# First weights of the second input pair cast first, the gates' pair put first, and sums and transfers moved

## The chip, the cores and the metric

The kernel runs on one core of a Trainium2 chip. The metric is the device time of one execution in microseconds; the kernel before took 1771.07, 1772.54 and 1774.09 us in three runs, with a median of 1772.54. The engines named here are PE (TensorE, matmul), DVE (VectorE), ACT (ScalarE), POOL (GpSimd) and SP (SyncE, which only issues transfers). Each runs its own instructions in the order in which they were written for it, and waits for the others by semaphores.

## The reference

One step of one layer of a streaming encoder is computed for a prompt of 1024 frames and a sample of 32 frames that share the weights; the model's width is 1024. All is in float32.

```python
h = rms_norm(x, g_mix)
z = h @ w_in
q, k, v, ch, cb, cc, ga, gb = jnp.split(z, SPLITS, axis=-1)
a = attn_core(q, k, v) @ w_attn_out          # windowed attention, 16 heads of 64
u = cc * ch
up = jnp.concatenate([conv_left, u], axis=1)
conv = up[:, 0:n] * conv_w[0]                # three taps
...
bo = (cb * conv) @ w_conv_out
x = x + (jax.nn.sigmoid(ga) * a + jax.nn.sigmoid(gb) * bo) @ w_mix_out
hc = rms_norm(x, g_cross)
...                                          # attention over 256 memory tokens
x = x + co @ w_co
hm = rms_norm(x, g_mlp)
x = x + jnp.square(jax.nn.relu(hm @ w_up)) @ w_down
```

A final norm follows. The tables of keys, values and convolution rows are outputs as well.

## The kernel before, in words

**Frames and products.** The 1056 frames are three chunks of 384, 384 and 288 columns. Features lie on the 128 partitions, in eight blocks. A weight tile is 128 x 1024. A float32 product is made of three passes in a faster format: a weight is split into a high part wh (a cast on ACT, line 120) and the rest wl (a subtraction on DVE, line 121), the activations likewise, and PE adds hi·hi, hi·lo and lo·hi (lines 175 to 177, 877 to 879, 1690 to 1692). So a weight is fetched by SP (wr), cast by ACT, subtracted by DVE, and then used by PE. The tiles wh and wl have three buffers each, wr two.

**Input pairs.** The columns of w_in after queries, keys and values are taken in 15 pairs of tiles (the list XP): C, H and B are the convolution's three inputs, a and b the two gates. A pair's product with chunks 0 and 1 is formed with seven block products instead of eight. For that, sums of weights are made (pair_sums: L866 and L869 give the sum s31, L867 and L868 the sum s24) and sums of operands (x_sums, lines 816 to 823, whose tiles xk are split into the tiles tk and X1 by x_split, lines 834 to 838). A pair has four weight products to be cast: 1 and 2 from the raw weights, 3 and 4 from the sums. Chunk 2 goes plainly into an accumulator pa. The functions x_p1 and x_p2 form the two halves of the first product; between them ACT copies the first half (L920) and the accumulator is then added to. The function x_start begins pairs 0 and 1 while attention ends; x_pair does the rest, and its marks "B11", "W1", "W4", "W3" and "W2" are the places where x_steps casts the next pair's weights.

**What is put into other stages.** The down projection also works with weight sums. They are made in memory beside the attention stage: SP copies tiles (L733), and POOL issues 40 transfers that add to them (L736, list adds), in one slot of attention after the other; each waits for the one before that it builds on. Up pairs (w_up, with key "u") go like input pairs: there, all four instructions of pair_sums were on POOL. In the down projection fold and refold (L1516 to L1526) load operands by POOL's queue, subtract, and store them again, in nine steps that are tied to the products around them.

**What sets the order.** A scheduler with a time model orders each engine's instructions when the program is built; those in pin keep their order. So an edit at one place can move rows in other stages too.

Of the kernel before, what the change touches and what calls it, by code (L numbers as in the profile page):

```python
# [38 lines left out]
def hybrid_step(ctx: ExitStack, tc: tile.TileContext, io):  # L39
    nc = tc.nc  # L40
    act, dve, pool_e, pe, sp = nc.scalar, nc.vector, nc.gpsimd, nc.tensor, nc.sync
# [3 lines left out]
    def nm(s):  # L45
        uid[0] += 1
        return f"{s}_{uid[0]}"
# [399 lines left out]
    def do_K(pr, extras=()):  # L447
        def fn(w):
            kt = at_tile([P, NT], F32, "kt")
            ktt[pr] = kt  # L450
            for c, (o, n) in enumerate(CH):
                a = acc_tile([P, n])
                gemm(a, w, xg[c])
                dve.tensor_mul(kt[:, o : o + n], a, R[c])
                after(extras, c)
            sp.dma_start(io["o_k"][pr], kt[:, 896:])

        return fn
# [22 lines left out]
    def do_Q(kv, j, extras=()):  # L481
        def fn(w):
            for c, (o, n) in enumerate(CH):
                npr = min(n, NPR - o)
                if j == 0:
                    qs[kv, c] = at_tile([P, 4, npr], F32R, "QA" if c < 2 else "QB", 2 if c < 2 else 1)
                    if n > npr:
                        qs[kv, 3] = at_tile([P, 4, n - npr], F32R, "QC", 2)
                a = acc_tile([P, n])
                gemm(a, w, xg[c])  # L490
                t = tmp(n)
                dve.scalar_tensor_tensor(t, a, 0.125, R[c], op0=ALU.mult, op1=ALU.mult)
                parts = [(qs[kv, c], slice(0, npr))]
                if n > npr:
                    parts.append((qs[kv, 3], slice(npr, n)))
                for q, s in parts:
                    for e in range(2):
                        own, other = slice(64 * e, 64 * e + 64), slice(64 - 64 * e, 128 - 64 * e)
                        h = 2 * j + e
                        act.copy(q[own, h], t[own, s])  # L500
                        dve.tensor_sub(q[other, h], t[own, s], q[own, h].bitcast(F32))
                after(extras, c)

        return fn
# [184 lines left out]
    def in_col(tile):  # L689
        which, f = tile  # L690
        return 10 + 8 * "HBCab".index(which) + f
# [34 lines left out]
    def at(slot, fn):  # L726
        events.setdefault(slot, []).append(fn)
# [14 lines left out]
    adds = [x for s in range(len(sums) + 2) for ph in (2, 1, 0) if 0 <= s - ph < len(sums) for x in sums[s - ph][1][ph]]  # L742
# [12 lines left out]
            at(base + 11, lambda kv=kv: do_KS_rest(kv + 1))  # L755
    for i, x in enumerate(copies):
        at(2 + i, x)
    for i, x in enumerate(adds):
        at(8 + i, x)
    at(38, lambda: x_raw(0))  # L760
    at(40, lambda: x_sums(0))
    at(42, lambda: x_raw(1))
# [2 lines left out]
    for i, h in enumerate(h for stage in hosts for h in stage):  # L765
        extras = [(c, e) for c in range(2) for e in events.get(3 * i + c + 1, [])]
        pre = events.get(3 * i, [])
        if h[0] == "Q":
            fn, key = do_Q(h[1], h[2], extras), qt(h[1], h[2])
        elif h[0] == "K":  # L770
            fn, key = do_K(h[1], extras), ("w_in", 8 + h[1])
        else:
            fn, key = do_in(h, extras), ("w_in", in_col(h))
# [28 lines left out]
    def x_raw(k):  # L802
        if k == 0:
            two = [at_tile([P, NT], F32R, t, 2).bitcast(F32) for t in ("KSh", "KSl")]
        elif k == 1:
            two = [C["pool"].tile([P, 1060], F32, tag="u", name=nm("u")), at_tile([P, 4, 256], F32, "bias").rearrange("p h k -> p (h k)")]
        else:
            two = [S["xk"].tile([P, 768], F32, tag="xk", bufs=4, name=nm("xk")) for _ in range(2)]
        xr[k] = b12, b22, b11, b21 = [t[:, a : a + 384] for t in two for a in (0, 384)]
        for t, c, f in ((b12, 1, k), (b22, 1, k + 4), (b11, 0, k), (b21, 0, k + 4)):  # L810
            sp.dma_start(t, io[f"x{c}"][:, f])
# [48 lines left out]
    def pair_sums(key):  # L860
        r1, r2 = raws[key]
        a, b = slice(0, 512), slice(512, 1024)
        s31 = PW["pool"].tile([P, 1024], F32, tag="s31", name=nm("s31"))
        s24 = PW["pool"].tile([P, 1024], F32, tag="s24", name=nm("s24"))
        side = dve if key[0] == "x" else pool_e
        side.tensor_tensor(s31[:, b], r2[:, a], r2[:, b], op=ALU.add)  # L866
        pool_e.tensor_tensor(s24[:, a], r1[:, a], s31[:, b], op=ALU.add)  # L867
        pool_e.tensor_tensor(s24[:, b], r1[:, b], s24[:, a], op=ALU.add)  # L868
        side.tensor_tensor(s31[:, a], r1[:, a], r2[:, a], op=ALU.add)  # L869
        raws[key] += [s31, s24]  # L870
# [13 lines left out]
        issue_w()  # L884


    XP = [((w, f), (w, f + 1)) for f in (2, 4, 6) for w in "CHB"]
    XP.insert(3, (("b", 4), ("b", 5)))
    XP += [(("b", 6), ("b", 7))] + [(("a", f), ("a", f + 1)) for f in (0, 2, 4, 6)]
    LATE = 3  # L890
    xs1, xemit = {}, {}

    def x_fetch(i):
        if i < len(XP):
            pair_fetch(("x", i), *(io["w_in"][in_col(t)] for t in XP[i]))

    def x_issue(i, which):
        if i < len(XP):
            pair_issue(("x", i), which)
        elif which != 2:  # L900
            resume()
# [6 lines left out]
    def x_put(i, half, c, v):  # L908
        tile = XP[i][half]
        if (i, half) not in xemit:  # L910
# [58 lines left out]
    def x_steps(i):  # L969
        if i == 0:  # L970
            todo = {"B11": lambda: x_issue(1, 4), "W4": lambda: x_issue(1, 3), "W2": lambda: [x_issue(1, 2), x_fetch(2), x_issue(2, 1)]}
        elif i == 1:
            todo = {"W4": lambda: x_issue(2, 4), "W3": lambda: x_issue(2, 3), "W2": lambda: x_issue(2, 2)}
        else:
            todo = {f"W{k}": lambda k=k: x_issue(i + 1, k) for k in (1, 4, 3, 2)}
            todo["B11"] = lambda: x_fetch(i + 1)

        def after(what):
            todo.get(what, lambda: None)()
            if what == "B11" and XP[i][0][0] == "a" and "cv_cm" in S:  # L980
                closed(S.pop("r2_cm"))
                closed(S.pop("cv_cm"))
                G["pool"] = ctx.enter_context(tc.tile_pool(name="gb", bufs=5, reuse_waits="tile", side="right"))

        return after

    def x_start():
        x_issue(0, 4)
        A = x_p1(0)
        x_issue(0, 3)  # L990
        x_c2(0, 0)
        x_p2(0, A)
        x_issue(1, 1)
        x_c2(0, 1)
        A = x_p1(1)
        x_p2(1, A)
        x_c2(1, 0)
# [391 lines left out]
    b11, b21, b22 = (lambda k: xm[0][k]), (lambda k: xm[0][k + 4]), (lambda k: xm[1][k + 4])  # L1389
# [125 lines left out]
    def refold(step):  # L1515
        if step % 2 == 0:  # L1516
            if fold:
                for to, k in (("n3", "b22"), ("n1", "b12"), ("t2", "b11"), ("n4", "b21")):
                    pool_e.dma_start(op_d[to][:, step // 2 - 1], fold[k])
            if step < 8:  # L1520
                for k in ("b12", "b22", "b11", "b21"):
                    fold[k] = H["pool"].tile([P, 384], F32, tag="fold", bufs=4, name=nm("fold"))
                    pool_e.dma_start(fold[k], op_d[k][:, step // 2])
        else:
            for to, x, y in (("b22", "b12", "b22"), ("b12", "b11", "b12"), ("b11", "b11", "b22"), ("b21", "b21", "b11")):
                pool_e.tensor_tensor(fold[to], fold[x], fold[y], op=ALU.subtract)  # L1526
# [251 lines left out]
    C11, C12, C21, C22 = (0, 0), (1, 0), (0, 4), (1, 4)  # L1778
    steps = [(j, t) for j in range(4) for t in range(2)]
# [13 lines left out]
    def twos(half, t):  # L1793
        return [h2_of(half, k) for k in range(8 * t, 8 * t + 8)]

    def beside_two(w, kind, then, half, f, begin, more=(), each=None, steps=steps, apart=False):

        for n, (j, t) in enumerate(steps):
            if (j, t) == (3, 1) and more:
                item(lambda: wanted.__setitem__(slice(0, 0), more))  # L1800

            def fn(ws, j=j, t=t, n=n):
                prod(kind, j, t, then)(ws)
                pump(pace(13 - 2 * n))
                if each:
                    each(n)
                two(half, j, t, f, begin, apart)(ws)
                pump(pace(12 - 2 * n))

            item(fn, ("w_down", w, j, t))  # L1810

    def alone(w, kind, then, begin=True, end=True, more=None):
        for j, t in steps:
# [6 lines left out]
            if more and (j, t) == (1, 0):  # L1820
# [1 line left out]

    want(twos(0, 1), ops("b21"))
    beside_two(0, "b11", ((*C12, True, False), (*C21, False, False), (*C22, False, False), (*C11, True, False)), 0, 0, True,
               twos(1, 0), lambda n: n > 3 and refold(n - 4), [(0, 0), (1, 0), (0, 1), (1, 1)] + steps[4:])
    want(twos(1, 1), ops("n4")[4:], ops("n4")[:4])
    beside_two(1, "b21", ((*C11, True, True),), 1, 0, False, each=lambda n: n < 5 and refold(n + 4))
    want(ops("t2"))
    beside_two(3, "n4", ((*C21, True, False),), 1, 4, True, apart=True)
    want(ops("n3"))  # L1830
# [128 lines left out]
```

## Time and profile before

| What | Value |
|---|---|
| Time of the runs, median (lowest to highest) | 1772.54 us (1771.07 to 1774.09) |
| The profiled execution's own time | 1774.1 us |
| Its span in the profile | 1772.3 us |
| Mean granted clock of PE | 0.995 |
| PE busy | 1735.1 us (98%) |
| DVE, ACT, POOL busy | 1203.3, 845.6, 580.0 us |

The span runs from the first to the last recorded work; the profiled execution's own time has 1.8 us around it. A row of a timeline gives start, duration, engine, line, operation, written and read tiles, shape, how many rows were put together, and in brackets the idle time ahead and what ended it. In a row of waits stand who waited, for which engine's write, the sum in us, how often, and the longest one.

### The profile page before, as it was taken

Reading aid. Unit: us, or ns where it says so; the run is one execution under the profiler, and the core shown is the slowest. Engines: PE = TensorE matmul, PEld = TensorE weight load, DVE = VectorE, ACT = ScalarE, POOL = GpSimd, SP = SyncE. Lnnn points to the kernel's source line nnn. Section 1 sums busy time; section 2 is a strip of 40 time slices with the busy share of each in tenths; the row PEclk is TensorE's granted clock in tenths of the full one; section 3 lists DMA queues with packets and bytes.
Section 4 is the critical chain, followed back from the end, with each engine's and each line's share of the span. In section 5 each row is a group of like instructions: output and inputs, shape, how many; then the busy total and the mean of one; then the engine's idle time right before and its main releaser. Section 6 shows DMA issues by size and latency. Waiting matters only on the chain.

```text
span 1772.3 us, 29923 instructions
## 1 busy us (share of the span) xinstructions
PE 1735.1 (98%) x11012; PEld 1714.5 (97%) x11012; DVE 1203.3 (68%) x2114; ACT 845.6 (48%) x1625; POOL 580.0 (33%) x602
## 2 busy tenths in 40 slices
PE   8999999999999999999999999999999999999997
PEld 8999999999999999999999999999999989999997
DVE  6768878677686767457566877676666676444764
ACT  8667767853232335234465755632222343432553
POOL 2245564553232310003324242375555352100111
PEclk9999999999999999999999999999999999999998
DMA  5428997771211325578766777744434496444673
GB/s 183 157 94 237 252 234 197 168 189 56 96 65 56 113 71 187 165 252 297 250 218 210 238 240 227 268 152 147 139 127 138 160 307 219 163 149 141 222 245 128
DMA packets 148547, 317.21 MB, mean 179 GB/s; under 512 B 18320, under 2 KB 101040, under 8 KB 147760
## 3 DMA queue, kind: packets, MB, share of 16 engines
q1 hardware_dynamic: 140448, 287.98, 48.5%
q0 software_dynamic: 7808, 27.27, 7.7%
q8 instruction: 87, 1.43, 0.3%
q14 instruction: 60, 0.49, 0.1%
q10 hardware_dynamic: 144, 0.05, 0.0%
HBM read 254.20 MB, written 98.78 MB: 199 GB/s over the span
## 4 chain that ended last, share of the span: by engine, by line
PE 78%; DMA 7%; DVE 6%; ACT 4%; issue 3%; POOL 2%; SPq 0%; POOLq 0%; DVEq 0%; ACTq 0%
PE acc L175 9%; PE acc L176 9%; PE acc L177 9%; PE acc L877 7%; PE acc L878 7%; PE acc L879 7%; PE acc L1692 5%; PE acc L1690 5%; PE acc L1691 5%; PE pa L176 3%; PE pa L177 3%; PE pa L175 3%; DVE wl L121 2%; DMA ct<-bc_d 1%; PE pt L587 1%
## 5 line engine op out<-in xcount | busy, mean ns | idle before, releaser
L120 ACT CAST wh<-wr 128x1024 fp32r<-128x1024 f32 (+1 forms) x224 | 234.3, 1046 | 312.2 <-PE acc L1691 89.0
L121 DVE TENSOR_TENSOR wl<-wr,wh 128x1024 fp32r<-128x1024 f32 (+1 forms) x224 | 306.9, 1370 | 103.7 <-ACT wh L120 102.4
L175 PE MATMUL acc<-Y,wh 128*128 128x384 f32 (+1 forms) x624 | 201.7, 324 | 0.7 <-DVE ct L1333 0.4
L176 PE MATMUL acc<-Y,wh 128*128 128x384 f32 (+1 forms) x624 | 201.9, 323 | 0.0
L177 PE MATMUL acc<-Y,wl 128*128 128x384 f32 (+1 forms) x624 | 201.7, 323 | 0.0
L175 PE MATMUL acc<-X,wh 128*128 128x384 f32 (+1 forms) x528 | 172.5, 327 | 0.1
L176 PE MATMUL acc<-X,wh 128*128 128x384 f32 (+1 forms) x528 | 171.3, 324 | 1.0 <-DVE X L256 1.0
L177 PE MATMUL acc<-X,wl 128*128 128x384 f32 (+1 forms) x528 | 171.0, 324 | 0.0
L252 POOL TENSOR_TENSOR xacc<-xacc,ct 128x384 f32<-128x384 f32 (+1 forms) x62 | 78.1, 1260 | 270.1 <-ACT ct L250 267.7
L175 PEld LDWEIGHTS acc<-Y,wh 128*128 128x128 f32 x624 | 117.2, 188 | 1.3 <-DVE ct L1333 0.7
L177 PEld LDWEIGHTS acc<-Y,wl 128*128 128x128 f32 x624 | 117.3, 188 | 0.0
L176 PEld LDWEIGHTS acc<-Y,wh 128*128 128x128 f32 x624 | 117.2, 188 | 0.0
L577 POOL TENSOR_SCALAR S<-S,rec 128x256 f32<-128x256 f32 (+1 forms) x96 | 90.3, 956 | 80.9 <-DVE rec L574 80.9
L1692 PE MATMUL acc<-Y,wl 128*128 128x384 f32 (+1 forms) x352 | 113.1, 321 | 2.6 <-DVE wl L121 2.6
L1690 PE MATMUL acc<-Y,wh 128*128 128x384 f32 (+1 forms) x352 | 113.1, 321 | 0.6 <-ACT wh L120 0.6
L1691 PE MATMUL acc<-Y,wh 128*128 128x384 f32 (+1 forms) x352 | 113.0, 321 | 0.0
L120 ACT CAST wh<-s 128x1024 fp32r<-128x1024 f32 x54 | 56.6, 1051 | 107.1 <-PE acc L878 69.6
L176 PEld LDWEIGHTS acc<-X,wh 128*128 128x128 f32 x528 | 100.0, 189 | 2.7 <-DVE X L256 1.8
L175 PEld LDWEIGHTS acc<-X,wh 128*128 128x128 f32 x528 | 99.9, 189 | 1.7 <-ACT wh L120 0.3
L177 PEld LDWEIGHTS acc<-X,wl 128*128 128x128 f32 x528 | 99.8, 189 | 0.6 <-DVE wl L121 0.2
L1118 POOL TENSOR_TENSOR sgl<-sgl,ct 128x384 f32<-128x384 f32 (+1 forms) x21 | 22.2, 1055 | 224.5 <-DVE sgl L1115 166.5
L121 DVE TENSOR_TENSOR Y<-ct,Y 128x384 fp32r<-128x384 f32 (+1 forms) x128 | 71.6, 591 | 31.4 <-ACT Y L120 31.0
(413 smaller groups left out, 5321.0 us busy)
## 6 DMA issues: line engine op xcount, KB each, us to landing
wr<-in_w_in SPq DMA_DIRECT2D x55, 512.0 KB, 3.4
wr<-in_w_up SPq DMA_DIRECT2D x48, 512.0 KB, 3.7
wsum_d<-in_w_down SPq DMA_DIRECT2D x32, 512.0 KB, 6.4
wr<-in_w_down SPq DMA_DIRECT2D x32, 512.0 KB, 3.5
wr<-wsum_d SPq DMA_DIRECT2D x32, 512.0 KB, 3.5
wl<-wl_d SPq DMA_DIRECT2D x28, 512.0 KB, 4.8
wsum_d<-in_w_down POOLq DMA_DIRECT2D x24, 512.0 KB, 7.9
wr<-in_w_conv_out SPq DMA_DIRECT2D x24, 512.0 KB, 4.7
```

Source lines behind the costliest of these rows:

```text
L120: act.copy(hi, src)
L121: dve.tensor_sub(lo, src, hi.bitcast(F32))
L175: pe.matmul(out, wh[:, a], hi, start=(k == 0), stop=False)
L176: pe.matmul(out, wh[:, a], lo, start=False, stop=False)
L177: pe.matmul(out, wl[:, a], hi, start=False, stop=(k == len(acts) - 1))
L577: pool_e.tensor_scalar_mul(stl[:, h, :nk], stl[:, h, :nk], rec[:, h : h + 1])
L877: pe.matmul(acc, wh[:, a], hi, start=(start and k == 0), stop=False, skip_group_check=True)
L878: pe.matmul(acc, wh[:, a], lo, start=False, stop=False, skip_group_check=True)
L879: pe.matmul(acc, wl[:, a], hi, start=False, stop=(k == 3), skip_group_check=True)
L1690: pe.matmul(a, wh[:, s], hi, start=(start and k == 0), stop=False, skip_group_check=True)
L1691: pe.matmul(a, wh[:, s], lo, start=False, stop=False, skip_group_check=True)
L1692: pe.matmul(a, wl[:, s], hi, start=False, stop=(stop and k == len(acts) - 1), skip_group_check=True)
```

## The change

It has five edits:

- x_start casts the first weights of pair 1 before all else, and the third weights of pair 0 only after pair 0's two halves.
- In the list XP, the pair of gate tiles (b4, b5) becomes pair 0; the three pairs C, H and B of tiles 2 and 3 become 1 to 3. The other pairs keep their places.
- Of the 40 transfers that add to the sums of w_down, the first 30 stay in attention's slots; the last ten are issued one each at the end ("W2") of input pairs 1 to 10.
- For up pairs 0 and 1, L866 and L869 are on DVE and no longer on POOL; L867 and L868 stay on POOL.
- The steps of refold begin one product later.

```diff
-    for i, x in enumerate(adds):
-        at(8 + i, x)
+    for i in range(30):
+        at(8 + i, adds.pop(0))
...
-        side = dve if key[0] == "x" else pool_e
+        side = dve if key[0] == "x" or key[1] < 2 else pool_e
...
-    XP = [((w, f), (w, f + 1)) for f in (2, 4, 6) for w in "CHB"]
-    XP.insert(3, (("b", 4), ("b", 5)))
+    XP = [(("b", 4), ("b", 5))]
+    XP += [((w, f), (w, f + 1)) for f in (2, 4, 6) for w in "CHB"]
...
             todo.get(what, lambda: None)()
+            if i and what == "W2" and adds:
+                adds.pop(0)()
...
     def x_start():
+        x_issue(1, 1)
         x_issue(0, 4)
         A = x_p1(0)
-        x_issue(0, 3)
         x_c2(0, 0)
         x_p2(0, A)
-        x_issue(1, 1)
+        x_issue(0, 3)
         x_c2(0, 1)
         A = x_p1(1)
         x_p2(1, A)
...
-               twos(1, 0), lambda n: n > 3 and refold(n - 4), [(0, 0), (1, 0), (0, 1), (1, 1)] + steps[4:])
+               twos(1, 0), lambda n: n > 4 and refold(n - 5), [(0, 0), (1, 0), (0, 1), (1, 1)] + steps[4:])
...
-    beside_two(1, "b21", ((*C11, True, True),), 1, 0, False, each=lambda n: n < 5 and refold(n + 4))
+    beside_two(1, "b21", ((*C11, True, True),), 1, 0, False, each=lambda n: n < 6 and refold(n + 3))
```

Two lines are added ahead of x_start, so line numbers above 980 are higher by two after the change.

**ACT, at the start of the input pairs.** Before, the cast of pair 1's first weights (wh_5149 from the raw tile wr_5046) stands here, among the casts of operand sums; the last row is the next weight cast of pair 0 or 1, of a sum s:

```order
L120 CAST wh_5083<-s_936_4982 128x1024
L120 CAST wh_5102<-s_935_4981 128x1024
L920 COPY s_960_5100<-acc_5087 128x384
L834 CAST tk_4881<-xk_4864 128x384
L834 CAST X_945_5034<-xk_4864 128x384
L834 CAST tk_4885<-xk_4863 128x384
L834 CAST tk_4889<-xk_4863 128x384
L834 CAST tk_4993<-xk_4870 128x384
L834 CAST tk_4997<-xk_4869 128x384
L120 CAST wh_5149<-wr_5046 128x1024
```

After the change (the same cast is wh_5073 from wr_5036) it stands in the attention stage, ahead of the first operand sums' casts:

```order
L604 COPY tO_4707<-o_4701 64x512
L120 CAST PTh_888_4720<-pt_4718 128x128
L120 CAST wh_5073<-wr_5036 128x1024
L834 CAST X_903_4815<-KSl_4253 128x384
L677 ACTIVATE ct_4938<-ct_4938 128x288
```

and farther down, where it stood, comes the third cast of pair 0 (wh_5141 from the sum s_935), followed by two sigmoids (L677) and the copy of pair 1's first half:

```order
L834 CAST tk_4987<-xk_4860 128x384
L120 CAST wh_5141<-s_935_4971 128x1024
L834 CAST X_947_5028<-xk_4861 128x384
L834 CAST tk_4991<-xk_4860 128x384
L677 ACTIVATE ct_5137<-ct_5137 128x384
L677 ACTIVATE ct_5170<-ct_5170 128x288
L920 COPY s_971_5187<-acc_5174 128x384
```

So the cast of pair 1 moved ahead by some 25 rows, and the casts of pair 0's third weights and the copies are now behind sigmoids of the gates.

**PE, at the same place.** Before, after the end of pair 0 (pa_5153) there are two rows of pair 1's first product and two of its chunk 2, and then the products with tk begin:

```order
L176 MATMUL pa_5153<-X_105_580,wh_955_5079 128x288
L177 MATMUL pa_5153<-X_104_579,wl_956_5080 128x288
L877 MATMUL acc_5181<-X_10_173,wh_5149 128x384
L878 MATMUL acc_5181<-X_11_174,wh_5149 128x384
L175 MATMUL pa_5212<-X_90_551,wh_5149 128x288
L176 MATMUL pa_5212<-X_91_552,wh_5149 128x288
L877 MATMUL acc_5251<-tk_4812,wh_5083 128x384
```

After, all 48 rows of pair 1's first product (acc_5174, both halves) and its chunk 2 (pa_5204) stand ahead of the products with tk. These are the last rows of them:

```order
L176 MATMUL pa_5204<-X_105_580,wh_5073 128x288
L177 MATMUL pa_5204<-X_104_579,wl_5074 128x288
L877 MATMUL acc_5174<-X_18_193,wh_5073 128x384
L878 MATMUL acc_5174<-X_19_194,wh_5073 128x384
L879 MATMUL acc_5174<-X_18_193,wl_5074 128x384
...
L879 MATMUL acc_5174<-X_24_205,wl_5074 128x384
L877 MATMUL acc_5242<-tk_4803,wh_5077 128x384
```

Pair 1's first product is no longer split around the products with tk.

**POOL, at the sums of the second up pair.** Before, all four of them stand here:

```order
L1408 TENSOR_TENSOR xacc_9095<-xacc_9095 128x384
L866 TENSOR_TENSOR s_2711_13861<-wr_2679_13621 128x512
L869 TENSOR_TENSOR s_2711_13861<-wr_13620,wr_2679_13621 128x512
L1340 TENSOR_TENSOR ct_13813<-ct_13811 128x288
L867 TENSOR_TENSOR s_2712_13862<-wr_13620,s_2711_13861 128x512
L1408 TENSOR_TENSOR xacc_9095<-xacc_9095 128x384
L868 TENSOR_TENSOR s_2712_13862<-wr_13620,s_2712_13862 128x512
```

and after, two:

```order
L1410 TENSOR_TENSOR xacc_9091<-xacc_9091 128x384
L867 TENSOR_TENSOR s_2712_13858<-wr_13616,s_2711_13857 128x512
L1342 TENSOR_TENSOR ct_13809<-ct_13807 128x288
L868 TENSOR_TENSOR s_2712_13858<-wr_13616,s_2712_13858 128x512
L1410 TENSOR_TENSOR xacc_9091<-xacc_9091 128x384
```

L866 and L869 have gone to DVE's queue; what is left of the pair's sums on POOL follows the addition to xacc at once. The fold's rows (L1516 to L1526) stand in the same order among the others as before, on PE, POOL and SP.

## The prediction

> **What bounds the kernel now.** I read the page first, then the waits of PE (columns: who waited, for whom, us in total, times, longest), then stretches of time.
>
> ```profile
> PE 1735.1 (98%) x11012; PEld 1714.5 (97%) x11012; DVE 1203.3 (68%) x2114; ACT 845.6 (48%) x1625; POOL 580.0 (33%) x602
> ```
>
> ```profile
> PE acc L877 <- ACT wh L120: 5.6, 3, 3.6
> ...
> PE o L599 <- DVE AO L606: 0.9, 1, 0.9
> ```
>
> TensorE is busy in 1735.1 of 1772.3 us and the change leaves its work as it is: as many matmuls, of the same shapes. So only PE's 37 us of idle time and its clock can move. The top row says that a weight cast on ScalarE is the costliest wait: three times, 3.6 us the longest. I looked for the place (columns: stretch, its length, busy us and instructions of PE, PEld, DVE, ACT, POOL, granted PE clock, DMA share, GB/s):
>
> ```profile
> 385.00:390.00 5.00, 1.91 (x13) 1.68 (x11) 5.00 (x7) 1.37 (x3) 2.39 (x3) 0.96 0.55 100
> 390.00:395.00 5.00, 4.45 (x14) 4.45 (x15) 5.00 (x7) 1.68 (x4) 4.82 (x4) 0.50 0.04 8
> 395.00:400.00 5.00, 5.00 (x26) 5.00 (x26) 2.07 (x3) 1.01 (x3) 3.23 (x3) 0.85 0.29 105
> 400.00:405.00 5.00, 5.00 (x36) 5.00 (x35) 0.52 (x2) 0.48 (x1) 0.31 (x2) 1.00 0.00 0
> ```
>
> The stall is at the start of the input pairs, and the next stretch shows a second loss that no wait lists: the clock is 0.50. PE, one by one:
>
> ```profile
> 386.62 0.29 PE L177 MATMUL pa<-X,wl 128*128 128x288 f32 x1
> 390.56 0.69 PE L877 MATMUL acc<-X,wh 128*128 128x384 f32 x1 [3.64 <-ACT wh L120]
> ...
> 391.84 0.52 PE L877 MATMUL acc<-tk,wh 128*128 128x384 f32 x1
> ...
> 396.32 0.41 PE L879 MATMUL acc<-tk,wl 128*128 128x384 f32 x1
> 396.57 0.34 PE L877 MATMUL acc<-tk,wh 128*128 128x384 f32 x1
> ...
> 398.66 0.33 PE L879 MATMUL acc<-X,wl 128*128 128x384 f32 x1
> ```
>
> From 396.57 to 398.66 are 12 steps, 0.174 us each. From 391.84 to 396.57 are 15 steps of the same shape, 4.73 us where 2.61 would do: 2.12 lost. The four matmuls between 390.56 and 391.84 (two of 384 columns, two of 288, together 0.62 at full rate) took 1.28: 0.66 lost. The stall thus costs 3.64 + 2.78 = 6.4 us. Why the cast is late, on ScalarE and VectorE:
>
> ```profile
> 388.63 0.92 ACT L834 CAST tk<-xk 128x384 fp32r<-128x384 f32 x2 [4.79 <-DVE xk L822]
> 389.46 1.04 ACT L120 CAST wh<-wr 128x1024 fp32r<-128x1024 f32 x1
> ```
>
> ```profile
> 387.46 1.14 DVE L822 SCALAR_TENSOR_TENSOR xk<-xk,prm,xk 128x384 f32<-128x384 f32 x1
> 388.99 0.68 DVE L866 TENSOR_TENSOR s<-wr 128x512 f32<-128x512 f32 x1
> ```
>
> The cast needs nothing from VectorE; it stands behind two casts of tk that wait 4.79 us for L822, and VectorE is busy 5.00 of 5.00 us there.
>
> **The change part by part.** *First weights first, gates first (x_start, XP).* The order rows ahead of this show wh of pair 1 cast behind the last PTh cast, where ScalarE was near 364 us. Its raw weights were fetched long before:
>
> ```profile
> 339.17 0.38 SPq L845 DMA_DIRECT2D wr<-in_w_in  x1
> ```
>
> So the 3.64 wait and the slow clock behind it go: −6.4. By 386.77 PE has done the same of pair 0 as now, and goes straight on with pair 1: 12 matmuls of 384 columns, 24 of 288 (0.13 each by their columns), 12 of 384, 7.3 us in all, and reaches the tk products near 394.1.
>
> What is late next? Those last 12 (near 392.0) add to an accumulator that ScalarE's L920 must have copied first. That copy now stands behind the cast of wh for pair 0's W3, two tk casts and two sigmoids, and the second sigmoid waits for a VectorE product that stands behind wl of W3. The rows this hangs on:
>
> ```profile
> 379.70 1.98 ACT L120 CAST wh<-s 128x1024 fp32r<-128x1024 f32 x2
> 381.71 0.48 ACT L920 COPY s<-acc 128x384 f32<-128x384 f32 x1
> ```
>
> ```profile
> 383.37 1.37 DVE L821 SCALAR_TENSOR_TENSOR xk<-xk,prm,xk 128x384 f32<-128x384 f32 x1
> 384.67 2.03 DVE L121 TENSOR_TENSOR wl<-s,wh 128x1024 fp32r<-128x1024 f32 x1
> ```
>
> VectorE after L821 (384.7) runs two tk subtractions and a product (about 0.5 each), L822 and L823 (0.6 to 1.1 each): 387.6. Two casts on ScalarE (0.92) and the wh cast (1.04) end at 389.6; wl (1.2 to 2.0) ends at 390.9 to 391.7, the product at 391.3 to 392.1, sigmoid and copy about 1 us later: 392.2 to 393.0, an estimate. PE would wait 0.2 to 1.0 us; I take 0.4, near its lower end. If VectorE and GpSimd slow each other as in the 2.03 us row above, it is up to 2.6. The first product of pair 1's W4 comes at 398.7; By estimate L866 and L869 follow wl on VectorE until 393.4, GpSimd's two sums end near 395.5, the cast near 396.6, wl at 397.8 to 398.6: in time, 0 taken. So **x_start: −6.0, between −6.4 and −3.8**.
>
> [...]
>
> *Ten adds of the w_down sums out of attention (adds).* PE waits 0.94 us in the attention stage for a VectorE that is held up by a load:
>
> ```profile
> 349.25 0.62 DVE L821 SCALAR_TENSOR_TENSOR u<-bias,prm,u 128x384 f32<-128x384 f32 x1 [4.03 <-DMA bias<-in_x]
> ```
>
> ```profile
> 352.08 0.47 PE L599 MATMUL o<-PTh,VS 128*128 128x512 f32 x1 [0.94 <-DVE AO L606]
> ```
>
> L606, for which PE waits, stands two instructions behind. The load competes with the adds that now come later, and has to land 0.94 us sooner for all of the wait to go. Bounds 0 and −0.94; −0.7, nearer the full end since 0.94 is little beside the 4.03 that L821 waits. Where the adds go:
>
> ```profile
> 450.00:800.00 350.00, 350.00 (x2194) 350.00 (x2193) 231.71 (x325) 121.27 (x180) 54.11 (x50) 1.00 0.39 127
> ```
>
> ```profile
> POOL s L867 <- issue: 98.3, 8, 17.8
> ```
>
> ```profile
> L736 POOL DMA_DIRECT2D wsum_d<-in_w_down x24: 794/870/1445, 143.5 to 385.6; - x24
> ```
>
> PE has no gap in these 350 us, GpSimd is busy 54 of them, and before the sums of a pair (L867) it idles 12 us on average (98.3 over 8, from 400 to 700 us). An add holds it 0.87 us (median of min/median/max in ns): hidden, 0. Without that cover ten would cost 8.7. The sums are read in the down projection, some 800 us later.
>
> *First up pairs' sums shared (side).* The wait at the second up pair:
>
> ```profile
> 1175.80 1.29 POOL L866 TENSOR_TENSOR s<-wr 128x512 f32<-128x512 f32 x1
> 1177.05 1.28 POOL L869 TENSOR_TENSOR s<-wr,wr 128x512 f32<-128x512 f32 x1
> ```
>
> ```profile
> 1182.27 1.04 ACT L120 CAST wh<-s 128x1024 fp32r<-128x1024 f32 x1 [5.47 <-POOL s L868]
> ```
>
> ```profile
> 1183.37 0.44 PE L877 MATMUL acc<-hx,wh 128*128 128x384 f32 x1 [1.07 <-ACT wh L120]
> ```
>
> GpSimd loses 2.57 us ahead of L868; VectorE does the two in 0.68 each (the L866 row above). L868 comes up to 2.6 us sooner, the cast too: −1.07, bounds 0 and −1.07. The first pair's L866 now stands ahead of some of VectorE's Gb products at 1126, where PE waits already: +0.7 at most, +0.2 taken.
>
> *Fold one step later.* The fold's instructions stand in the same order with and without it on every engine: they are tied by their data. 0.
>
> *Down projection.* Nothing there is edited, but the rows move: two weight casts come two rows and one row later behind casts of H, and three fetches of weights one or two rows later behind ct loads.
>
> ```profile
> 1446.03 1.04 ACT L120 CAST wh<-wr 128x1024 fp32r<-128x1024 f32 x1
> ...
> 1461.38 1.06 ACT L120 CAST wh<-wr 128x1024 fp32r<-128x1024 f32 x1 [0.88 <-DMA wr<-in_w_down]
> ```
>
> ```profile
> 1449.30 0.44 PE L1692 MATMUL acc<-Y,wl 128*128 128x384 f32 x1 [1.56 <-DVE wl L121]
> ```
>
> One H cast more ahead of 1446.03 makes that cast some 0.46 us later (two such casts are 0.92 above), and the wait behind it grows by as much; a fetch of weights that the cast at 1461.38 already waits for, behind a late load, could make 2.5. The cast that another one leaves free comes sooner: −0.5 at the other end. I take +0.5, nearest to one cast.
>
> **Sum:** −6.0 − 0.7 − 1.07 + 0.2 + 0.5 = −7.1; ends −6.4 − 0.94 − 1.07 − 0.5 = −8.9 and −3.8 + 0.7 + 2.5 = −0.6. The profiled execution took 1774.1, span 1772.3; the runs have a median of 1772.54, 1.6 below it. 1774.1 − 7.1 = 1767.0 for such an execution, **1765.4 us** for the median.
>
> **Rivals.** *The idle only moves (A).* The L920 copy comes 2.5 to 4 us late because VectorE is saturated until 395. For it: DVE 5.00 of 5.00 in two stretches, and the new chain through wl, product and sigmoid; against: wl of pair 1 has left that stretch. Gain 6.4 − 3 + 1 = 4.4, 1768; past 3.6 us idle the slow clock returns as well and about 1 us is left: 1771.5.
>
> *The slow clock is not the idle's (B)*, but comes with this stretch. Against it: the matmul behind the wait of 1.56 us takes 0.44, not the 0.52 of the slow stretch. Gain 3.64 + 0.7: 1768.
>
> *Something given back in up and down (C):* the terms at their bad ends, gain 2 to 3: 1770.
>
> *The moved adds hold GpSimd (D), slower.* Each add waits for the one before to land, and L867 and L868 of a pair are queued behind it, then a cast, then PE.
>
> ```profile
> wsum_d<-in_w_down POOLq DMA_DIRECT2D x24, 512.0 KB, 7.9
> ```
>
> A pair is 132 matmuls, of 2194 in 350 us: 21 us long. At 7.9 us to land an add doesn't wait; it decides once landing takes 12 us more than a pair, about 33 us. Then every pair past that loses; 1.5 us on each of ten is +15, less 7: 1780. [...] Against it is the L736 row: never over 1.45 us.
>
> **Chances.** Forecast 0.68, A 0.18, B 0.05, C 0.04, D 0.05. Of A 0.10 gains over 0.2% (3.5 us, about what can be told from no change here), of B 0.04, of C 0.01; so faster 0.82, same 0.08 + 0.01 + 0.03 + 0.01 for the forecast's bad end = 0.13, slower 0.05. The sum's ends from the median are 1763.6 and 1771.9; the range goes 1.7 us lower, for the spread of the runs, and stops at 1771.0, with most of A and C in: 1761.9 to 1771.0.
>
> **What would show it.** Right: no wait over 1.5 us and clock 1.00 from 385 to 400; no PE wait on AO near 352, none on wh near 1183. A wait of PE on ScalarE's L920 copy, 0.2 to 1 us, near 392. Clock 0.50 without an idle above 3 us is B; L867 waiting behind L736 is D; new rows near 1450 and 1465 are C. I am wrong if the first tk product doesn't come 6 us sooner.

## The result, and the profile after

The changed kernel takes 1763.99 us (median of four runs, 1760.33 to 1765.63) against 1772.08 for the kernel before (four runs): a ratio of 0.995, 95% interval 0.9932 to 0.9969. That is 8.1 us less. The profiled execution took 1763.26 us, its span 1761.5, mean granted clock 0.995. In line numbers above 980 two have to be taken off to find them in the kernel printed above.

The page's first part and two rows of PE's waits, after:

```profile
PE 1734.7 (98%) x11012; PEld 1714.6 (97%) x11012; DVE 1202.1 (68%) x2118; ACT 846.8 (48%) x1625; POOL 575.6 (33%) x594
```

```profile
PE acc L1693 <- DVE H L121: 1.9, 4, 0.7
...
PE acc L877 <- ACT wh L120: 0.5, 1, 0.5
```

PE's work is the same (every kernel here has the three passes, so what a product in another format takes isn't shown); its idle time went from 37.2 to 26.8 us (1761.5 − 1734.7). The row that was the top one, PE waiting for a weight cast (5.6 us), is down to 0.5, and the wait on AO is gone from the list. Pair 1's first weights are now cast in the attention stage:

```profile
362.57 1.05 ACT L120 CAST wh<-wr 128x1024 fp32r<-128x1024 f32 x1 [1.74 <-PE acc L176]
```

and the start of the input pairs reads so (the same stretches as before; columns as there):

```profile
385.00:390.00 5.00, 5.00 (x36) 5.00 (x35) 4.96 (x9) 3.94 (x8) 2.29 (x2) 1.00 0.20 69
390.00:395.00 5.00, 5.00 (x32) 5.00 (x31) 2.29 (x3) 2.33 (x4) 4.92 (x5) 1.00 0.12 33
395.00:400.00 5.00, 5.00 (x30) 5.00 (x30) 2.17 (x2) 0.00 (x0) 0.63 (x1) 1.00 0.29 105
400.00:405.00 5.00, 4.35 (x26) 4.03 (x25) 3.88 (x7) 2.13 (x3) 0.43 (x1) 1.00 0.00 0
```

Where 1.91 and 4.45 of 5 us were busy at clocks of 0.96 and 0.50, PE is now busy throughout at clock 1.00; the first gap, 0.65 us, comes at 401.70.

To see where in the program time goes, PE's 11012 matmuls of a trace were put in order of time and the n-th of them set beside the n-th of the trace of before (median over 17 neighbours). The table gives the difference in us at times of before's trace; a step from one line to the next is what that stretch gained (down) or lost (up). The second column is another execution of the changed kernel, the rest are the experiments below.

| before's time | after | after, again | start + gates | adds | sums | after less sums | late fold, less sums |
|---|---|---|---|---|---|---|---|
| 349.6 | −0.5 | −0.1 | 1.5 | −0.1 | 0.3 | −0.5 | 0.5 |
| 353.4 | −1.7 | −1.3 | 1.3 | −1.2 | −0.8 | −1.6 | −0.7 |
| 385.9 | −1.6 | −1.2 | 1.3 | −1.2 | −0.8 | −1.6 | −0.6 |
| 412.2 | −7.7 | −7.2 | −4.0 | −3.5 | 0.1 | −7.6 | −6.6 |
| 825.2 | −8.4 | −8.0 | −4.8 | −3.5 | 0.0 | −8.4 | −7.2 |
| 832.3 | −10.2 | −9.9 | −6.7 | −5.0 | −1.8 | −10.3 | −8.0 |
| 1114.5 | −11.2 | −9.9 | −6.6 | −4.2 | −2.3 | −10.6 | −7.9 |
| 1208.6 | −9.9 | −9.2 | −6.6 | −2.8 | −1.9 | −10.9 | −7.3 |
| 1431.8 | −9.9 | −9.2 | −6.6 | −2.7 | −1.7 | −10.8 | −7.3 |
| 1444.6 | −5.6 | −9.4 | −5.1 | −1.7 | −1.6 | −10.2 | −9.4 |
| 1471.2 | −9.3 | −11.3 | −6.6 | −1.2 | −3.3 | −11.0 | −13.2 |
| 1755.4 | −9.3 | −11.3 | −6.6 | −1.2 | −3.3 | −11.0 | −13.2 |

The change gains 1.2 us at the attention wait (349.6 to 353.4) and 6.1 at the start of the input pairs (385.9 to 412.2). Nearly all columns gain 1 to 2 us more between 825 and 832, the kernel with an unchanged order (below) too: there the profiled execution of before had 1.3 us of waits that no other profile has:

```profile
828.44 0.45 PE L175 MATMUL acc<-M,wh 128*128 128x384 f32 x1 [0.44 <-ACT M L120]
829.76 0.44 PE L176 MATMUL acc<-M,wh 128*128 128x384 f32 x1 [0.88 <-DVE M L121]
```

That isn't the change's, nor are the 1.5 to 1.8 us by which every other profile is shorter than before's behind the last matmul (the span of after is 10.8 us shorter, where the table ends at −9.3). With these two, before's 1774.1 lies 2.0 us above the median of 1772.08.

### The profile page after: what moved, and what is told of

Its sections match the earlier page's. It is cut to its first block, busy times and chain, and to the rows that moved or that the text cites. A ratio compares the mean times of both kernels' runs of the same rounds, so it can differ in the third digit from the quotient of the medians.

```text
span 1761.5 us, 29915 instructions
## 1 busy us (share of the span) xinstructions
PE 1734.7 (98%) x11012; PEld 1714.6 (97%) x11012; DVE 1202.1 (68%) x2118; ACT 846.8 (48%) x1625; POOL 575.6 (33%) x594
## 4 chain that ended last, share of the span: by engine, by line
PE 88%; DMA 4%; DVE 3%; ACT 2%; issue 2%; POOL 1%; SPq 0%; POOLq 0%; DVEq 0%; ACTq 0%
PE acc L175 11%; PE acc L176 11%; PE acc L177 11%; PE acc L877 7%; PE acc L879 7%; PE acc L878 7%; PE acc L1693 6%; PE acc L1694 6%; PE acc L1692 6%; PE pa L176 3%; PE pa L175 3%; PE pa L177 3%; PE pt L587 2%; DMA wr<-in_w_up 1%; DVE wl L121 1%
## 5 line engine op out<-in xcount | busy, mean ns | idle before, releaser
L121 DVE TENSOR_TENSOR Y<-ct,Y 128x384 fp32r<-128x384 f32 (+1 forms) x128 | 67.4, 559 | 36.9 <-ACT Y L120 36.2
```

Source lines behind the costliest of these rows:

```text
L121: dve.tensor_sub(lo, src, hi.bitcast(F32))
```

## The experiments

The kernel before had medians of 1772.73, 1771.40 and 1772.89 us in the three sessions. Each ratio is to it, in the same session.

**The start of the input pairs together (start + gates).** Before with the new order of x_start and the new XP:

```diff
-    XP.insert(3, (("b", 4), ("b", 5)))
+    XP = [(("b", 4), ("b", 5))]
+    XP += [((w, f), (w, f + 1)) for f in (2, 4, 6) for w in "CHB"]
...
+        x_issue(1, 1)
         x_issue(0, 4)
         A = x_p1(0)
-        x_issue(0, 3)
         x_c2(0, 0)
         x_p2(0, A)
-        x_issue(1, 1)
+        x_issue(0, 3)
```

> The kernel before with two edits alone: the new x_start and the gates' pair first. Theory (stage by stage): the stall of 3.64 us on the late cast and the slow clock behind it are one loss of 6.4 us, and these two edits alone remove it; median 6 to 7.5 us below before, clock 1.00 from 385 to 400 us, the 0.94 us wait near 352 still there, 1.07 at the second up pair still there. Rival: the ten moved adds are needed for the gain too, since POOL and the transfers make VectorE late there; then at most 4 us. In the prediction ScalarE's copy of pair 1's first half was to cost PE 0.2 to 1.0 us.

Measured: 1765.98 us, 0.9965 (0.9952 to 0.9977). PE's only wait from 385 to 412 us is this one; it stands in the changed kernel as well, at 401.70:

```profile
405.30 0.44 PE L877 MATMUL acc<-X,wh 128*128 128x384 f32 x1 [0.65 <-DVE lt L950]
```

The clock is 1.00 from 385 to 400 us. Most of the change's gain is this.

**The two apart.** First only the order of x_start, then only XP:

```diff
+        x_issue(1, 1)
         x_issue(0, 4)
...
+        x_issue(0, 3)
         x_c2(0, 1)
```

> The kernel before with the new x_start alone; the first pair stays C2, C3. Theory: the early cast of pair 1's first weights is what removes the stall, so most of the two edits' gain of 6.2 us is here: 5 to 7 us below before, no wait on that cast. Rival: the gates' pair first is needed too, since the convolution's products keep VectorE and POOL busy at that place and another wait of 1 to 3 us takes the stall's place; then 2 to 4 us below before.

Measured: 1770.38 us, 0.9995 (0.9981 to 1.0009). The stall isn't gone, it has moved. PE, then the stretch around it, then POOL in this kernel:

```profile
405.73 0.45 PE L877 MATMUL acc<-tk,wh 128*128 128x384 f32 x1 [1.57 <-ACT wh L120]
406.99 0.69 PE L879 MATMUL acc<-tk,wl 128*128 128x384 f32 x1 [0.64 <-DVE wl L121]
```

```profile
405.00:410.00 5.00, 3.63 (x11) 3.31 (x12) 2.75 (x4) 1.19 (x2) 1.01 (x1) 0.66 0.29 108
```

```profile
392.06 0.81 POOL L736 DMA_DIRECT2D wsum_d<-in_w_down  x1
392.98 1.05 POOL L629 TENSOR_TENSOR Ga<-Ga,R 128x288 f32<-128x288 f32 x1
396.13 1.26 POOL L629 TENSOR_TENSOR Ga<-Ga,R 128x384 f32<-128x384 f32 x1 [2.10 <-DVE Ga L628]
...
401.96 1.28 POOL L867 TENSOR_TENSOR s<-wr,s 128x512 f32<-128x512 f32 x1
403.32 1.28 POOL L868 TENSOR_TENSOR s<-wr,s 128x512 f32<-128x512 f32 x1
```

PE now waits for pair 1's fourth weights: their sum on POOL (L867, L868) stands behind a transfer, splits of operand sums (L838) and the products of L629, one of which waits 2.10 us for VectorE. This is the longest of the ten executions, 1775.64 us: ahead of the edit's place it has lost 5.2 us on before already, with a wait of 2.36 on AO at 355.86. So it shows which wait comes next, not what a median execution gains.

```diff
-    XP = [((w, f), (w, f + 1)) for f in (2, 4, 6) for w in "CHB"]
-    XP.insert(3, (("b", 4), ("b", 5)))
+    XP = [(("b", 4), ("b", 5))]
+    XP += [((w, f), (w, f + 1)) for f in (2, 4, 6) for w in "CHB"]
```

> The kernel before with the gates' pair first alone; x_start as before. Theory: the cast still stands behind the tk casts and these wait for VectorE, so the stall stays (3 us or more, clock 0.50 behind it): within 1.5 us of before. Rival: gates need less of VectorE at the start of the pairs than the convolution's products, so the tk chain and the cast are earlier, the idle falls under some 2 to 3 us, the clock stays up: 3 to 5 us below before.

Measured: 1771.48 us, 1.0002 (0.9987 to 1.0017); the stall is as it was:

```profile
391.36 0.69 PE L877 MATMUL acc<-X,wh 128*128 128x384 f32 x1 [4.05 <-ACT wh L120]
```

So neither part alone is worth anything that can be measured (the intervals reach some 3 us either way), and the two together are worth 6.8 us by their medians. In the changed kernel the same two sums follow the operands' sums with nothing of L629 or L736 between, and the cast is in time:

```profile
390.77 1.75 POOL L867 TENSOR_TENSOR s<-wr,s 128x512 f32<-128x512 f32 x1
392.60 1.29 POOL L868 TENSOR_TENSOR s<-wr,s 128x512 f32<-128x512 f32 x1
```

They start some 11 us sooner. Of these 6.8 are only that the one execution is 5.2 us behind before's at 385.9, and the other 1.6 ahead; the remaining 4 or so are the order.

**The changed kernel with the old XP**, to see whether moving the adds does for the start what the gates do:

```diff
-    XP = [(("b", 4), ("b", 5))]
-    XP += [((w, f), (w, f + 1)) for f in (2, 4, 6) for w in "CHB"]
+    XP = [((w, f), (w, f + 1)) for f in (2, 4, 6) for w in "CHB"]
+    XP.insert(3, (("b", 4), ("b", 5)))
```

> The changed kernel with C2, C3 as pair 0 again (no gates' pair first). From the run of the new x_start alone: GpSimd's three products L629 of the convolution stand ahead of the sums L867, L868 of pair 1, so PE waits for the cast of the fourth weights. Theory: that is the gates' whole part; a wait of 1 to 2.5 us on that cast is back near 400 us, and the time is 2 to 5 us above the changed kernel. Rival: with the ten adds out of the way GpSimd has room enough; within 1 us of the changed kernel.

Measured: 1766.74 us, 0.9969 (0.9954 to 0.9983); the changed kernel, run again beside it (its text below), had 1764.85, 0.9962 (0.9949 to 0.9974). In its trace the stretch from 385.9 to 412.2 gains 4.7 us instead of 6.1, with a wait of 0.64 for wl at 398.49 and none for the cast. The intervals overlap: start with adds has most of what start with gates has, and the rest, about 2 us, isn't settled.

> The changed kernel as it is, once more, as the base for the three runs beside it: 1762 to 1766 us. If the slow stretch of PE's clock in its down projection (near 1428 to 1433 us in the first profile) belongs to this order of instructions, it is there again; if it was one execution's, it isn't.

**Is the slow clock the idle time's?** (rival B). Before, with the second half of pair 0's chunk 2 computed twice, so that PE has 24 more matmuls of 288 columns to do in the idle (3.1 us at 0.13 each; the first result is overwritten):

```diff
-    def x_c2(i, half):
+    def x_c2(i, half, again=False):
...
         gemm(a, x_w(i, 1 + half), xg[2])
+        if again:
+            gemm(a, x_w(i, 1 + half), xg[2])
...
-        x_c2(0, 1)
+        x_c2(0, 1, again=True)
```

> The kernel before, but chunk 2 of pair 0's second tile is multiplied twice in x_start (24 more matmuls of 288 columns, 3.2 us, the same result), so that PE works through most of its idle 3.64 us without anything else moving. Theory (the slow clock follows from the idle time): the wait on the cast falls to about 0.4 us, the clock stays 1.00 from 390 to 400, the products with tk run at 0.174 us each: 2 to 3 us below before with more work done. Rival (the slow clock comes with this stretch, from transfers or power, whatever PE did before): clock 0.50 again, time as before or up to 0.5 us more.

Measured: 1766.93 us, 0.9979 (0.9968 to 0.999): faster with more work. This kernel's PE and its stretches:

```profile
391.54 0.44 PE L877 MATMUL acc<-X,wh 128*128 128x384 f32 x1 [0.74 <-ACT wh L120]
394.43 0.45 PE L878 MATMUL acc<-tk,wh 128*128 128x384 f32 x1 [0.24 <-DVE tk L836]
397.66 0.44 PE L879 MATMUL acc<-X,wl 128*128 128x384 f32 x1 [1.62 <-DVE wl L121]
```

```profile
390.00:395.00 5.00, 4.02 (x24) 3.30 (x22) 5.00 (x7) 2.42 (x5) 3.85 (x3) 1.00 0.23 45
395.00:400.00 5.00, 3.38 (x20) 3.06 (x20) 3.43 (x4) 1.57 (x4) 4.24 (x4) 1.00 0.23 80
```

The wait on the cast is 0.74, the clock 1.00, and the stretch is the same one, with VectorE as saturated until 395. B falls: before, the clock was 0.50 behind 3.64 us of idle, and in the same stretch it is 1.00 where 0.74 us of it are left. How the whole gain comes about isn't shown. Two more waits follow here, so that the idle is 2.60 instead of 3.64 and the added work takes 3.1; this execution (1771.39, the second-longest of the ten) gains only 0.3 us from 385.9 to 412.2, set beside before's matmul by matmul without the 24. No trace shows one near the median.

**The adds alone:**

```diff
-    for i, x in enumerate(adds):
-        at(8 + i, x)
+    for i in range(30):
+        at(8 + i, adds.pop(0))
...
+            if i and what == "W2" and adds:
+                adds.pop(0)()
```

> The kernel before with one edit alone: the last ten adds issued in the input pairs. Theory: the load that VectorE waits for near 342 us lands sooner, the 0.94 us wait of PE near 352 goes, nothing is lost in the pairs (PE without a gap there, L867 never held by an add): median 0.7 to 1.3 us below before. Rival (the adds hold GpSimd): gaps of PE in the pairs, median above before by up to 15 us. Second rival (the wait at 352 isn't the adds'): no change, 0.94 stays.

Measured: 1769.01 us, 0.9978 (0.9969 to 0.9987), some 3.7 us where 0.7 was predicted. The wait at 352 us goes (1.1 in the table), and part of the big stall's cost goes with it, without an edit there:

```profile
387.73 0.44 PE L877 MATMUL acc<-X,wh 128*128 128x384 f32 x1 [2.04 <-ACT wh L120]
391.22 0.44 PE L878 MATMUL acc<-tk,wh 128*128 128x384 f32 x1 [0.85 <-DVE tk L836]
394.47 0.44 PE L879 MATMUL acc<-X,wl 128*128 128x384 f32 x1 [0.43 <-DVE wl L121]
```

```profile
385.00:390.00 5.00, 2.96 (x18) 2.73 (x18) 5.00 (x6) 2.64 (x5) 3.77 (x4) 1.00 0.00 0
390.00:395.00 5.00, 3.72 (x20) 2.91 (x19) 4.88 (x6) 1.43 (x4) 5.00 (x4) 1.00 0.00 0
```

The wait on the cast is 2.04 instead of 3.64, and the clock stays at 1.00. Two waits follow that before doesn't have, so that the idle is 3.32 in all; the 2.3 us that this stretch gains in the table are thus mostly the clock's. The casts of tk ahead of the first wait, which wait for VectorE, come 2.8 us sooner, 1.6 more than the 1.2 by which all is earlier (why VectorE gets there sooner wasn't tried by itself):

```profile
385.80 0.92 ACT L834 CAST tk<-xk 128x384 fp32r<-128x384 f32 x2 [3.27 <-DVE xk L822]
```

Start with gates and adds thus remove the same stall, and their gains don't add: 6.8 and 3.7 alone, 8.1 for all five edits. For the attention wait, the load that L821 waited 4.03 us for holds it up 0.19 in the changed kernel:

```profile
345.22 0.62 DVE L821 SCALAR_TENSOR_TENSOR u<-bias,prm,u 128x384 f32<-128x384 f32 x1 [0.19 <-DMA bias<-in_x]
```

and in the pairs the ten cost nothing. The 350 us in which they now stand, after:

```profile
450.00:800.00 350.00, 350.00 (x2193) 350.00 (x2192) 236.89 (x335) 122.84 (x181) 66.24 (x64) 1.00 0.48 144
```

GpSimd is busy 12 us more, PE has no gap. Rival D falls.

**The sums alone, and the change without them:**

```diff
-        side = dve if key[0] == "x" else pool_e
+        side = dve if key[0] == "x" or key[1] < 2 else pool_e
```

> The kernel before with one edit alone: two of the four sums of the first two up pairs on VectorE. The prediction's theory: the 1.07 us wait on wh at the second up pair goes, up to 0.2 comes back at the first pair, 0.5 is lost in the down projection: median 0.3 to 0.9 us below before. Rival, from the trace after the change: the wait only changes its name (on ScalarE's copy L1401 and VectorE's subtraction L1433 at the same places), and the down projection's weight casts come later: no gain in the up pairs, median 0 to 1.5 us above before.

> The changed kernel without the edit of the up pairs' sums. The prediction's theory: the 1.07 us wait is back, median about 0.4 us above the changed kernel (which is at 1764.0). Rival: that edit costs more than it brings, and this one is 0 to 2 us below the changed kernel; in the down projection the casts stand as in the kernel before, and the stretch from 1424 to 1434 us of the changed kernel with many short gaps and a clock of 0.61 to 0.71 isn't there.

Measured: alone 1771.67 us, 0.9998 (0.9988 to 1.0008); the change without them 1763.92, 0.9949 (0.9937 to 0.9961). They gain nothing that can be measured, though the intervals, some 2 us either way, wouldn't exclude the forecast 0.9. The traces do: the wait of 1.07 near 1183 has others in its place. The changed kernel at the first and the second up pair, and then the one without the sums' edit:

```profile
1157.12 0.45 PE L877 MATMUL acc<-Y,wh 128*128 128x384 f32 x1 [0.75 <-ACT s L1403]
1172.95 0.45 PE L879 MATMUL acc<-hx,wl 128*128 128x384 f32 x1 [0.51 <-DVE wl L121]
1177.70 0.44 PE L877 MATMUL acc<-hx,wh 128*128 128x384 f32 x1 [0.65 <-DVE lt L1435]
```

```profile
1172.52 0.44 PE L877 MATMUL acc<-hx,wh 128*128 128x384 f32 x1 [1.35 <-ACT wh L120]
```

With the sums on DVE, it is wl and lt, written by DVE itself, that PE waits for at the second pair, 1.11 to 1.19 us together in all five profiles with the edit. At the first pair all five have a wait of 0.75 to 0.93 on ScalarE's copy (L1403), which is at most 0.20 without the edit. So by the traces the edit costs a little.

**The fold alone.** On every engine the rows stand in the same order as before:

```diff
-               twos(1, 0), lambda n: n > 3 and refold(n - 4), [(0, 0), (1, 0), (0, 1), (1, 1)] + steps[4:])
+               twos(1, 0), lambda n: n > 4 and refold(n - 5), [(0, 0), (1, 0), (0, 1), (1, 1)] + steps[4:])
...
-    beside_two(1, "b21", ((*C11, True, True),), 1, 0, False, each=lambda n: n < 5 and refold(n + 4))
+    beside_two(1, "b21", ((*C11, True, True),), 1, 0, False, each=lambda n: n < 6 and refold(n + 3))
```

> The kernel before with the fold's steps one later alone. The instructions and waits of every engine stand as in the kernel before, so both theories say no change; the difference that is measured, at most 1.5 us either way, is what an edit of no effect looks like, and its trace shows how far the stages of one program differ from one execution to another.

Measured: 1772.88 us, 1.0006 (0.9996 to 1.0017). Nothing, as the unmoved rows say.

**The fold really delayed.** In the changed kernel GpSimd loads the fold's operands as soon as they are in memory, and subtracts beside VectorE's splits of H, for which PE waits: 1.9 us in the list above. So the first four loads were made to wait for the last H tile, by a copy of one element per partition into the tile that the load then overwrites; once on the changed kernel, and once without the sums' edit.

```diff
                     fold[k] = H["pool"].tile([P, 384], F32, tag="fold", bufs=4, name=nm("fold"))
+                    if step == 0:
+                        pool_e.tensor_copy(fold[k][:, 0:1], h2[0][15][1][:, 0:1].bitcast(F32))
```

> The changed kernel, but the fold really starts later: four one-element copies on GpSimd from the last H tile of the first half are put ahead of its first loads, so these wait until that tile has been split. Theory: the fold's loads and GpSimd's subtractions are what makes the H tiles late in the down projection (their splits take 0.8 to 0.9 us where 0.46 is usual); PE's waits on H and the slow clock near 1430 us shrink, 1.5 to 4 us below the changed kernel. Rival: H waits for its own loads (six ct buffers, SP's queue); then the waits stay and the time is within 1 us of the changed kernel, or above it where the fold now collides with something later.

> The same later fold in the changed kernel without the edit of the up pairs' sums. Theory: as the run beside it, 1.5 to 3 us below the changed kernel, since the up pairs' edit was worth nothing; this would be a version faster than both. Rival: within 1 us of the changed kernel.

Measured: with the sums 1762.55 us, 0.994 (0.9928 to 0.9952); without them **1758.62 us, 0.9919 (0.9908 to 0.9931)**, 14.3 us less than before and 6.2 less than the changed kernel in the same session. It beats both. Its gate on GpSimd (L1526 is the added copy, L1527 the loads), VectorE's splits, SP's loads, and the stretch:

```profile
1429.14 1.19 POOL L1526 COPY fold<-H 128x1 f32<-128x1 f32 x4 [12.57 <-DVE H L121]
1430.27 2.27 POOL L1527 DMA_DIRECT2D fold<-b_d  x4
```

```profile
1423.45 2.15 DVE L121 TENSOR_TENSOR H<-ct,H 128x288 fp32r<-128x288 f32 x5 [0.76 <-ACT H L120]
```

```profile
1418.96 5.31 SPq L1510 DMA_DIRECT2D ct<-hid_d  x7
```

```profile
1415.00:1450.00 35.00, 35.00 (x227) 34.84 (x226) 25.24 (x43) 17.98 (x34) 13.02 (x21) 1.00 0.90 301
```

and without the gate, the changed kernel less the sums' edit:

```profile
1420.77 5.64 DVE L121 TENSOR_TENSOR H<-ct,H 128x288 fp32r<-128x288 f32 x6 [2.15 <-ACT H L120]
```

```profile
1415.00:1450.00 35.00, 31.97 (x203) 30.71 (x202) 25.38 (x37) 16.68 (x32) 19.88 (x26) 1.00 0.90 309
```

A split of H takes 0.43 us with GpSimd quiet and 0.94 beside its subtractions, the seven loads span 5.31 us (8.96 without the gate), and PE has no gap where it had 3.0 us. From 1431.8 to 1471.2 the table gives 5.9 us for the gate, 0.2 without it. Up to 1435 us the rows of PE, DVE, ACT and SP stand in the same order in both kernels, and GpSimd's differ by the fold's alone, so it is the delay that does it. Whether the subtractions on GpSimd or the fold's transfers weigh more wasn't separated. With the sums' edit the gain is smaller (1762.55): there PE waits 0.84 us for a weight cast at 1437.64 and 1.16 for a wl at 1439.42, and the clock is 0.50 for 3.4 us from 1439.2.

## Why the prediction came out, point by point

- **The start of the input pairs, −6.0: right, 6.1 in the trace, but for the pair of edits, not for the order of x_start.** On before's times the fourth weights' sum was to end near 395.5 and wl at 397.8 to 398.6; they ended at 393.9 and 396.7, with all of PE 1.6 us ahead: 395.5 and 398.3. The new wait on the copy L920 (+0.4) didn't come: the copy ended 0.7 us ahead of its matmul. The cast ahead of wl ended at 387.21, with those 1.6 us at 388.8 instead of the estimated 389.6, and wl took 1.22 us, the low end. After, these four rows:

```profile
387.30 1.22 DVE L121 TENSOR_TENSOR wl<-s,wh 128x1024 fp32r<-128x1024 f32 x1
...
395.01 1.70 DVE L121 TENSOR_TENSOR wl<-s,wh 128x1024 fp32r<-128x1024 f32 x1 [1.69 <-ACT wh L120]
```

```profile
389.26 0.46 ACT L920 COPY s<-acc 128x384 f32<-128x384 f32 x1
```

```profile
390.44 0.34 PE L877 MATMUL acc<-X,wh 128*128 128x384 f32 x1
```

  The step that failed is unspoken: "W4 in time" was worked out for the changed order with the gates first, and nothing said that with the old XP L629 and the transfer stand ahead of L867. There rival A is what happens in the one execution that was traced: the idle moves, 1.57 us, and takes the clock along (0.66 from 405 to 410 us).
- **"I am wrong if the first tk product doesn't come 6 us sooner" was badly put.** It comes at 392.56, 0.7 later than before, since pair 1's 48 matmuls now stand ahead of it. The 6 us are seen at the end of pair 1.
- **The adds, −0.7: too small.** The wait was 0.94 in full (1.2 in the table). Alone they gain 3.7 since the stall's slow clock goes too (1.00 instead of 0.50 from 390 to 395 us); in the sum, that is gone already.
- **The sums, −1.07 + 0.2: wrong.** They gave nothing. The step that failed took the old wait as removed and didn't ask what is late next at the second pair, where two more instructions stand on DVE ahead of wl and lt: 1.11 to 1.19 us of waits in place of 1.07. Its cost at the first pair, +0.2 and at most +0.7 on Gb, was too small and at another wait, 0.75 to 0.93 on the copy L1403.
- **The fold, 0: right.**
- **The down projection, +0.5: not to be told.** From 1431.8 to 1471.2 one execution of the changed kernel lost 0.6, the other gained 2.1. What bounds this place was missed: the fold beside H's splits, not the weight casts' rows.
- **The sum.** −7.1 was forecast (1765.4), −8.1 measured (1763.99). Against the table the errors are −0.1 at the start, −0.5 at the adds and, taking the sums as nothing, +0.9 there; about −1.3 is left that no term has, the +0.5 of the down projection among it. So part of the closeness of the total is luck: a term that was wrong and one that was too small offset each other. Between executions of one program single stretches differ by more (below). Rivals B and D fell by their runs, A holds for x_start alone; of C, 1.3 us are given back in up here (1114.5 to 1208.6) and 0.7 in the other execution, with the waits of the sums' edit in both. The kernel with the adds alone gives back 1.4 there by another wait, 1.44 on VectorE's ct (L1335) at 1139.69.

## What to carry to other kernels

Before moving one late cast, follow the next cast of the same unit through every queue to its sum: an edit that only moves a stall is worth nothing until the instruction that would be late next is moved too (here 0.9995 for the order of x_start alone, 0.9965 with the gates). The fold's steps are tied by their data, and a later place in the program didn't delay them (1.0006); if such an operation disturbs a neighbour, make it wait for something (5.9 us from 1431.8 to 1471.2, by the table). And where several edits remove one stall, time them together and apart: here the gains didn't add, 6.8 and 3.7 alone, 8.1 for all five.

## What the runs showed that was not expected

**The clock dropped to 0.50 in a long wait, and elsewhere among short ones.** In stretches of 1 us, before, then after at the down projection, then with the order of x_start alone:

```profile
389.00:390.00 1.00, 0.00 (x0) 0.00 (x0) 1.00 (x3) 1.00 (x3) 0.00 (x0) 0.82 1.05 209
...
396.00:397.00 1.00, 1.00 (x6) 1.00 (x6) 1.00 (x2) 0.01 (x1) 1.00 (x1) 0.76 0.00 0
```

```profile
1426.00:1427.00 1.00, 0.34 (x2) 0.34 (x3) 1.00 (x2) 0.95 (x3) 0.92 (x2) 1.00 0.79 302
1427.00:1428.00 1.00, 0.60 (x4) 0.26 (x2) 1.00 (x2) 0.55 (x2) 0.98 (x3) 0.53 0.27 58
...
1433.00:1434.00 1.00, 1.00 (x5) 1.00 (x5) 0.22 (x1) 0.00 (x0) 0.00 (x0) 0.55 1.05 403
```

```profile
406.00:407.00 1.00, 0.36 (x3) 0.04 (x2) 1.00 (x2) 0.19 (x1) 0.00 (x0) 0.82 0.94 377
...
410.00:411.00 1.00, 1.00 (x7) 1.00 (x7) 0.00 (x0) 0.00 (x0) 0.00 (x0) 0.98 0.00 0
```

All the stretches left out have 0.50. With the edges' means split into 1.00 and 0.50 (0.82 is 0.36 us slow, 0.76 is 0.48), the slow stretches last 6.84, 6.84 and 3.40 us. The first one begins near 389.6, in the wait of 3.64 that ends at 390.56. In the changed kernel no gap in the 3 us ahead of the drop at 1427 was over 0.69 us:

```profile
1424.70 0.41 PE L1693 MATMUL acc<-H,wh 128*128 128x288 f32 x1 [0.34 <-DVE H L121]
1425.57 0.40 PE L1692 MATMUL acc<-H,wh 128*128 128x288 f32 x1 [0.34 <-ACT H L120]
1426.66 0.40 PE L1693 MATMUL acc<-H,wh 128*128 128x288 f32 x1 [0.69 <-DVE H L121]
```

Five matmuls start in these 3 us, and PE is busy for 1.64 of them (1.30 to 1426, 0.34 behind it). With the order of x_start alone the clock drops near 406.6, in a wait of 0.64 that comes behind one of 1.57. With the adds alone it stays at 1.00 from 385 to 395, at waits of 2.04, 0.85 and 0.43. So the longest single wait doesn't tell in these traces where the clock drops; what does wasn't shown. The 3 and 3.6 us of idle at which the prediction put the slow clock were estimates from before's one wait of 3.64, and these traces don't bear them out.

Nor does the idle time alone tell what such a place costs. From 1415 to 1450 PE is idle for 2.32 us here (35.00 − 32.68) at a mean clock of 0.90, and for 2.62 (35.00 − 32.38) at 1.00 in the other execution of this program. From 1431.8 to 1444.6 this one lost 4.3 us, the other none.

**Executions of one program differ in single stretches by 1 to 4 us** (the 1.3 us of waits near 829 that only one profile has, the H waits above), and in all by up to 11: 1767.81 to 1779.05 with the new XP alone, 1760.24 to 1767.85 in the changed kernel run again. A term under 1 us can't be read from one trace beside another.
